# Modulation tiles issued from ScalarE's queue one turn ahead, with the offset row earlier and smaller recurrence masks

## The chip, the cores and the metric

The program runs on one core of one Trainium2 chip. Its engines are TensorE (PE; PEld is its weight load), VectorE (DVE), ScalarE (ACT), GpSimd (POOL) and SyncE (SP), which here only issues transfers. Each engine works through its own instructions in the order in which they stand, and waits at an instruction until what it needs is there. The metric is the device time of one execution in microseconds (us), the median of several runs.

## The reference

One layer of a transformer-like trunk, for a sequence of 2048 tokens of width 1024, in float32. A conditioning vector c gives six modulation vectors; the change touches how four of them are computed.

```python
mod = silu(c) @ ada_w + ada_b            # 1024 -> 6 x 1024
sh1, sc1, g1, sh2, sc2, g2 = split(mod, 6)
h = rmsnorm(x, norm_mix_w) * (1 + sc1) + sh1
proj = h @ w_in                          # 1024 -> 3624
o_a = hgrn2_mixer(...)                   # 4 heads, gated linear recurrence
o_b = dsa_mixer(...)                     # index scores, top 256 keys, softmax
o_c = conv_module(...)                   # 31 taps, depthwise
x = x + g1 * (concat([o_a, o_b, o_c]) @ w_out)
h = rmsnorm(x, norm_mlp_w) * (1 + sc2) + sh2
x = x + g2 * (square(relu(h @ w1)) @ w2)
out = rmsnorm(x, final_norm_w)
```

The recurrence `S_t = diag(f_t) S_(t-1) + (1 - f_t) outer i_t` is computed in pieces of 128 tokens; inside a piece the causal weights are built up over levels of halves (1, 2, 4, ... 64 tokens), and a mask says which entries each level writes.

## The kernel before

The sequence is cut into 4 blocks of 512 tokens. A matmul in float32 is made of three in a rounded format: high parts by high parts, and two cross terms (`mm_T`, L418 to L429). Weights come from HBM as `wraw`, are split into `whi` and `wlo`, and are kept in HBM (`wk_d`) for the blocks that follow, which load them as `wk`.

The program is written as a main stream of matmuls (`in_block`, `out_block`, `mlp_block`) with background work in generators: `queues` holds the recurrence ("fast"), the modulation ("ada"), the convolution ("conv"), the index scores, the top-k search and the attention. After each unit of the main stream `step` gives every queue a credit (`rates`, 800 for "ada"), and `pump` runs its generator until the credit is used up. The framework's scheduler then puts all instructions in an order of its own for each engine by a model of their durations, within what the tiles' buffers and dependences allow, and adds the waits. So an edit in one place can move instructions of every engine.

`ada_gen` (L770 to L785) computes g1, sc2, sh2 and g2 in 16 parts of 256 columns. A part has 8 turns (`ada_part`, L192 to L200). Each turn issues a transfer of a tile of 128 rows by 256 columns of `ada_w` from SyncE's queue (L195), and VectorE multiplies it by a column of silu(c) and adds it to the sum `acc` (L197 for the first, L199 after). The tiles have tag `adw` with AB = 2 buffers. For g1 and g2 a matmul with ones (L777) sums over the partitions; then the row of the offset is loaded, into the tag `adw` too (L779), added by VectorE (L780), which also frees the PSUM bank, and stored (L781). For sc2 and sh2 `ada_col` (L202 to L208) does it by columns. The queue is filled in block 1 and emptied at "prep" in block 3; the scheduler takes its first tiles earlier.

`ada_half` (L216 to L248) does the same for sc1 and sh1 at the very start, with tiles of 512 columns on SyncE's queue, since the first matmul needs them (a1 and sh1, used in `to_act_steps`, L286 to L291).

`late_consts` makes `lmask`, 5 levels by 256 entries of one byte: four equal copies of 64 entries, one for each piece of 128 tokens (L511 to L520). `hgrn_gen` reads it in `copy_predicated` at L690 and L711.

Of the kernel before, what the change touches and what calls it, by code (L numbers as in the profile page):

```python
# [8 lines left out]
F32 = mybir.dt.float32  # L9
# [3 lines left out]
U8 = mybir.dt.uint8  # L13
# [65 lines left out]
def trunk(ctx, tc, x, c, ada_w, ada_b, norm_mix_w, norm_mlp_w, w_in, hg_lb_logits,  # L79
# [22 lines left out]
    def nm(s):  # L102
        uid[0] += 1
        return f"{s}_{uid[0]}"
# [86 lines left out]

    def ada_part(pool, wtag, wbufs, acc, sec, c0, w):  # L192
        for k in range(NK):
            t = pool.tile([P, w], F32, tag=wtag, bufs=wbufs, name=nm("adw"))
            (nc.gpsimd if AQ else nc.sync).dma_start(t, ada2[k * P:(k + 1) * P, sec * D + c0:sec * D + c0 + w])  # L195
            if k == 0:
                V.tensor_scalar(acc, t, cact[:, 0:1], None, op0=OP.mult)  # L197
            else:
                V.scalar_tensor_tensor(acc, t, cact[:, k:k + 1], acc, op0=OP.mult, op1=OP.add)  # L199
            yield 1.2 * w  # L200

# [259 lines left out]
    lbt = cst.tile([P, 4], F32, name="lbt")  # L461
    lmask = cst.tile([P, 5, 256], U8, name="lmask")

# [31 lines left out]
    def late_consts():  # L495
# [16 lines left out]
        for l in range(5):  # L512
            h = 1 << l
            ng = 128 // (2 * h)
            V.memset(mwork, 1.0)
            G.affine_select(mwork, mwork, pattern=[[0, 4], [-2 * h, ng], [0, h]],
                            compare_op=OP.is_ge, fill=0.0, base=0, channel_multiplier=1)
            G.affine_select(mwork, mwork, pattern=[[0, 4], [2 * h, ng], [0, h]],
                            compare_op=OP.is_gt, fill=0.0, base=h, channel_multiplier=-1)
            V.tensor_copy(lmask[:, l, :], mwork)  # L520

# [155 lines left out]
    def hgrn_gen(b, h, q, k, f, v, gate):  # L677
# [8 lines left out]
        for i in range(2):  # L686
            pv = pd[i][:, :384].rearrange("p (c n) -> p c n", c=2)
            V.tensor_tensor(at.rearrange("p (c n) -> p c n", c=4)[:, 2 * i:2 * i + 2], pv[:, :, :P],
                            ident[:, None, :].to_broadcast([P, 2, P]), OP.mult)
            V.copy_predicated(at.rearrange("p (c g two) -> p c g two", c=4, two=2)[:, 2 * i:2 * i + 2, :, 1],  # L690
                              lmask[:, 0, :128].rearrange("p (c g) -> p c g", c=2), pv[:, :, P:])
        V.tensor_tensor(qn, qn, f.rearrange("p (c n) -> p c n", c=4), OP.mult)
# [4 lines left out]
        for l in range(7):  # L697
# [9 lines left out]
            if 0 < l < 5:  # L707
                for cc in range(4):
                    T.matmul(ps[:, cc * 64:(cc + 1) * 64], k[:, cc * P:(cc + 1) * P],
                             qv[:, cc, :, 1, :], start=True, stop=True)  # L710
                V.copy_predicated(av[:, :, :, 1, :],  # L711
                                  lmask[:, l, :].rearrange("p (c g e) -> p c g e", c=4, e=hs), psv)
            elif l:
# [56 lines left out]
    def ada_gen():  # L770
        for sec, dst in ((2, None), (4, a2), (3, sh2), (5, None)):
            for c0 in range(0, D, AW):
                acc = hp.tile([P, AW], F32, tag="ada", bufs=1, name=nm("adacc"))
                yield from ada_part(hp, "adw", AB, acc, sec, c0, AW)
                if dst is None:
                    pt = ps_xp(13)
                    T.matmul(pt[:1, :AW], ones, acc, start=True, stop=True)  # L777
                    row = hp.tile([1, AW], F32, tag="adw", bufs=AB, name=nm("adrow"))
                    dma(row, ada_b[0:1, sec * D + c0:sec * D + c0 + AW])  # L779
                    V.tensor_tensor(row, pt[0:1, :AW], row, OP.add)  # L780
                    dma(g_d[sec][:, c0:c0 + AW], row)  # L781
                else:
                    ada_col(acc, sec, c0, AW, dst)
            if sec == 4:
                ada_scale(a2, "nmlp")  # L785


# [892 lines left out]
```

## Time and profile before

| | before |
|---|---|
| median of 3 runs, us | 2964.3 (2963.78 to 2969.74) |
| the profiled execution, us | 2959.47 |
| its span, us | 2957.7 |
| mean granted TensorE clock | 0.981 |
| bytes moved | 688.62 MB, mean 233 GB/s |

The page gives busy time by engine, 40 slices of the span, the chain of work that ended last and the costliest groups. Other views of the same execution list groups of instructions with what ended the idle time before them, who waited for whom ("A <- B: us in total, times, longest us"), one tile's instructions with who waits for them, stretches with busy time of each engine, and instructions in order of time. SPq is SyncE's queue. An instruction is named by engine, line and tile (written <- read).

### The profile page before, as it was taken

To read this page: it belongs to the slowest core of one execution; us is meant where nothing else is said; L and a number is where in the kernel's file an instruction comes from. 1 tells how busy PE (TensorE), PEld (TensorE's weight loads), DVE (VectorE), ACT (ScalarE), POOL (GpSimd) and SP (SyncE) were. 2 spreads that over 40 slices of the span, in tenths; PEclk is the share of its full clock that TensorE was granted. 3 is DMA by queue.
4 is the path that set the end of the run, shared out by engine and by line. 5 is a ranking of instruction groups with operands and counts; after the bars stand their busy time and mean duration, and the time that the engine had idled before them with its cause. 6 is when DMAs were issued, how large, how long until landed. Compare 5 with 4: busy or idle time off the path is not lost.

```text
span 2957.7 us, 42853 instructions
## 1 busy us (share of the span) xinstructions
PE 2796.6 (95%) x14116; PEld 2310.3 (78%) x14116; DVE 1680.2 (57%) x3450; ACT 1297.0 (44%) x2704; POOL 1241.9 (42%) x1163
## 2 busy tenths in 40 slices
PE   6998988998899989999998999999999999999998
PEld 4877877787788877788776888877788888778777
DVE  7684486967526354756849637385944221244555
ACT  4545354545314235556545544444553333233333
POOL 7574152225205155566646322224432223335454
PEclk9999999899999999999998999999999999999999
DMA  8976666575655577899978967767786667676676
GB/s 283 289 232 220 214 218 214 175 226 180 213 183 179 177 239 249 266 281 307 300 233 263 299 193 221 225 217 237 246 286 210 224 207 229 214 272 229 224 228 214
DMA packets 428075, 688.62 MB, mean 233 GB/s; under 512 B 43383, under 2 KB 171452, under 8 KB 427836
## 3 DMA queue, kind: packets, MB, share of 16 engines
q1 hardware_dynamic: 427680, 685.67, 72.0%
q8 instruction: 113, 1.85, 0.3%
q14 instruction: 126, 1.03, 0.1%
q10 hardware_dynamic: 156, 0.07, 0.0%
HBM read 532.74 MB, written 152.84 MB: 232 GB/s over the span
## 4 chain that ended last, share of the span: by engine, by line
PE 38%; DMA 5%; DVE 4%; POOL 2%; issue 1%; ACT 1%; SPq 0%; POOLq 0%; DVEq 0%; ACTq 0%
PE mm L1317 10%; PE mm L427 8%; PE ax L427 6%; PE ax L1317 5%; PE mm L1477 4%; PE po L1013 1%; PE at L979 1%; PE at L1001 1%; DMA wk<-wk_d 1%; PE at L1317 1%; PE ix L822 1%; DMA tr<-in_mlp_w_dram 1%; DMA xo<-x_d 1%; DMA wraw<-in_mlp_w_dram 1%; DMA out_dram<-xo 1%
## 5 line engine op out<-in xcount | busy, mean ns | idle before, releaser
L427 PE MATMUL mm<-ah,wk 128*128 128x512 f32 x1920 | 517.3, 401 | 15.1 <-ACT k L647 5.9
L427 PEld LDWEIGHTS mm<-ah,wk 128*128 128x128 f32 x1920 | 358.3, 191 | 90.0 <-ACT k L647 6.9
L321 POOL TENSOR_TENSOR wlo<-wraw,whi 128x512 fp32r<-128x512 f32 x210 | 287.3, 1388 | 215.0 <-ACT whi L320 87.9
L1011 POOL TENSOR_TENSOR pT<-L,pT 128x512 fp32r<-128x512 f32 (+3 forms) x160 | 194.7, 1219 | 297.3 <-ACT pT L1010 183.1
L829 DVE SCALAR_TENSOR_TENSOR s<-r,iw_s,s 128x512 f32<-128x512 f32 (+3 forms) x266 | 239.2, 899 | 117.1 <-ACT r L824 108.8
L427 PE MATMUL mm<-al,wk 128*128 128x512 f32 x960 | 262.1, 395 | 0.0
L981 DVE CUSTOM_DVE_ANT_0 L<-at,bias 128x512 f32<-128x512 f32 (+3 forms) x152 | 93.4, 618 | 210.8 <-PE at L979 173.6
L427 PEld LDWEIGHTS mm<-al,wk 128*128 128x128 f32 x960 | 178.9, 190 | 36.0
L824 ACT ACTIVATE r<-ix 128x512 f32<-128x512 f32 (+3 forms) x256 | 133.4, 554 | 162.1 <-PE ix L822 117.1
L273 POOL TENSOR_TENSOR hl<-hr,hh 128x512 fp32r<-128x512 f32 x96 | 128.4, 1338 | 175.1 <-ACT hh L265 174.5
L1317 PE MATMUL mm<-wk,hh 128*128 128x512 f32 x640 | 198.1, 399 | 0.9 <-DVE ah L290 0.4
L598 POOL TENSOR_TENSOR cside<-cside,ctap 128x512 f32<-128x512 f32 x112 | 150.3, 1342 | 100.5 <-ACT ctap L597 88.3
L427 PE MATMUL ax<-ah,wk 128*128 128x512 f32 x720 | 187.0, 393 | 1.5 <-ACT hc L1451 1.5
L320 ACT CAST whi<-wraw 128x512 fp32r<-128x512 f32 x210 | 121.3, 620 | 146.7 <-DMA wraw<-in_mlp_w_dram 55.0
L931 DVE TENSOR_SCALAR_CACHE_REDUCE cum<-s,ssm 128x384 bf16<-128x384 f32 (+13 forms) x112 | 165.4, 1476 | 7.8 <-POOL s L833 5.7
L427 PEld LDWEIGHTS ax<-ah,wk 128*128 128x128 f32 x720 | 134.0, 188 | 31.2 <-ACT hc L1451 1.9
L1477 PE MATMUL mm<-wk,hc 128*128 128x512 f32 x588 | 148.3, 397 | 2.9 <-DVE acc L1485 2.8
L995 ACT ACTIVATE L<-L,nmx 128x512 f32<-128x512 f32 (+3 forms) x160 | 103.8, 650 | 105.8 <-DVE nmx L990 105.5
L1009 ACT COPY L<-at 128x512 f32<-128x512 f32 (+3 forms) x160 | 82.9, 522 | 152.0 <-PE at L1001 150.5
L1317 PEld LDWEIGHTS mm<-wk,hh 128*128 128x128 f32 x640 | 117.9, 188 | 27.1 <-DMA wk<-wk_d 0.9
L1477 PEld LDWEIGHTS mm<-wk,hc 128*128 128x128 f32 x588 | 109.5, 188 | 33.2 <-DVE acc L1485 6.7
L1317 PE MATMUL ax<-wk,hh 128*128 128x512 f32 x384 | 123.4, 400 | 0.9 <-DMA wk<-wk_d 0.5
(367 smaller groups left out, 6338.0 us busy)
## 6 DMA issues: line engine op xcount, KB each, us to landing
wk<-wk_d SPq DMA_DIRECT2D x776, 256.0 KB, 4.5
wk<-wk_d SPq DMA_DIRECT2D x196, 512.0 KB, 5.2
wk_d<-whi SPq DMA_DIRECT2D x210, 256.0 KB, 4.1
wk_d<-wlo SPq DMA_DIRECT2D x210, 256.0 KB, 5.7
wraw<-in_mlp_w_dram SPq DMA_DIRECT2D x68, 512.0 KB, 5.6
kc<-sk_d SPq DMA_DIRECT2D x112, 256.0 KB, 3.0
vc<-v_d SPq DMA_DIRECT2D x112, 256.0 KB, 4.9
adw<-in_ada_w_dram SPq DMA_DIRECT2D x128, 128.0 KB, 2.9
```

The costliest lines, as they stand in the source:

```text
L273: e.tensor_tensor(lo[:, i:j], src[:, i:j], hi[:, i:j].bitcast(F32), OP.subtract)
L320: A.copy(hi, src)
L321: G.tensor_tensor(lo, src, hi.bitcast(F32), OP.subtract)
L427: T.matmul(ps, ww[k], aa[k], start=(n == 0 and k0 == 0), stop=(n == len(order) - 1 and k1 == NK))
L598: G.tensor_tensor(side, side, tap, OP.add)
L824: A.activation(r[:, :w], ps[:, :w], AF.Relu, scale=32.0 ** -0.5)
L829: V.scalar_tensor_tensor(s[:, c0:c0 + w], r[:, :w], iw, s[:, c0:c0 + w], op0=OP.mult, op1=OP.add)
L931: V.tensor_scalar(dump, s, t, -AIM - i * STEP, op0=OP.is_ge, op1=OP.add, accum_out=d)
L995: A.activation(lt[:, :w], lt[:, :w], AF.Exp, bias=nmx, accum_out=sm[:, cb:cb + 1])
L1011: G.tensor_tensor(pT[:, :nt, 1], lv, pT[:, :nt, 0].bitcast(F32), OP.subtract)
L1317: T.matmul(ps, aa[f][:, tok * P:(tok + 1) * P], ww[i], start=(first and n == 0), stop=(last and n == 5))
L1477: T.matmul(bank[t], aa[:, k, t * P:(t + 1) * P], ww[k], start=(i in (0, 2, 4) and n == 0), stop=(n == 5), skip_group_check=True)
```

## The change

Three edits. The tiles of `ada_gen` are issued from ScalarE's queue (`nc.scalar.dma_start`), and the tile of the next turn is fetched before VectorE's operation of this one; the tag keeps its two buffers. The row of the offset gets a tag of its own (`adr`, one buffer), is issued from ScalarE's queue as well, and at the start of a part and not at its end. `lmask` holds 5 x 64 entries, which L690 and L711 read through a repeated index.

```diff
--- before.py
+++ after.py
@@ -189,15 +189,10 @@
     def col(key, i=0, n=1):
         return cols[:, offs[key] + i:offs[key] + i + n]
 
-    def ada_part(pool, wtag, wbufs, acc, sec, c0, w):
-        for k in range(NK):
-            t = pool.tile([P, w], F32, tag=wtag, bufs=wbufs, name=nm("adw"))
-            (nc.gpsimd if AQ else nc.sync).dma_start(t, ada2[k * P:(k + 1) * P, sec * D + c0:sec * D + c0 + w])
-            if k == 0:
-                V.tensor_scalar(acc, t, cact[:, 0:1], None, op0=OP.mult)
-            else:
-                V.scalar_tensor_tensor(acc, t, cact[:, k:k + 1], acc, op0=OP.mult, op1=OP.add)
-            yield 1.2 * w
+    def ada_fetch(sec, c0, k):
+        t = hp.tile([P, AW], F32, tag="adw", bufs=AB, name=nm("adw"))
+        nc.scalar.dma_start(t, ada2[k * P:(k + 1) * P, sec * D + c0:sec * D + c0 + AW])
+        return t
 
     def ada_col(acc, sec, c0, w, dst):
         n = w // P
@@ -459,7 +454,7 @@
     lbc = cst.tile([P, 4], F32, name="lbc")
     oml = cst.tile([P, 4], F32, name="oml")
     lbt = cst.tile([P, 4], F32, name="lbt")
-    lmask = cst.tile([P, 5, 256], U8, name="lmask")
+    lmask = cst.tile([P, 5, 64], U8, name="lmask")
 
     zq = cst.tile([P, 14], F32, name="zq")
     gq_ = cst.tile([P, 14], F32, name="gq_")
@@ -517,7 +512,7 @@
                             compare_op=OP.is_ge, fill=0.0, base=0, channel_multiplier=1)
             G.affine_select(mwork, mwork, pattern=[[0, 4], [2 * h, ng], [0, h]],
                             compare_op=OP.is_gt, fill=0.0, base=h, channel_multiplier=-1)
-            V.tensor_copy(lmask[:, l, :], mwork)
+            V.tensor_copy(lmask[:, l, :], mwork[:, :64])
 
     def ev_index_k(b, ps):
         full = st("stg", STG)
@@ -688,7 +683,7 @@
             V.tensor_tensor(at.rearrange("p (c n) -> p c n", c=4)[:, 2 * i:2 * i + 2], pv[:, :, :P],
                             ident[:, None, :].to_broadcast([P, 2, P]), OP.mult)
             V.copy_predicated(at.rearrange("p (c g two) -> p c g two", c=4, two=2)[:, 2 * i:2 * i + 2, :, 1],
-                              lmask[:, 0, :128].rearrange("p (c g) -> p c g", c=2), pv[:, :, P:])
+                              lmask[:, 0, None, :].to_broadcast([P, 2, 64]), pv[:, :, P:])
         V.tensor_tensor(qn, qn, f.rearrange("p (c n) -> p c n", c=4), OP.mult)
         yield 1500
         fl = f
@@ -709,7 +704,7 @@
                     T.matmul(ps[:, cc * 64:(cc + 1) * 64], k[:, cc * P:(cc + 1) * P],
                              qv[:, cc, :, 1, :], start=True, stop=True)
                 V.copy_predicated(av[:, :, :, 1, :],
-                                  lmask[:, l, :].rearrange("p (c g e) -> p c g e", c=4, e=hs), psv)
+                                  lmask[:, l, :].rearrange("p (g e) -> p g e", e=hs)[:, None].to_broadcast([P, 4, gc, hs]), psv)
             elif l:
                 for i in range(gc):
                     r0 = 2 * hs * i
@@ -768,22 +763,38 @@
     AW = 256
 
     def ada_gen():
-        for sec, dst in ((2, None), (4, a2), (3, sh2), (5, None)):
-            for c0 in range(0, D, AW):
-                acc = hp.tile([P, AW], F32, tag="ada", bufs=1, name=nm("adacc"))
-                yield from ada_part(hp, "adw", AB, acc, sec, c0, AW)
-                if dst is None:
-                    pt = ps_xp(13)
-                    T.matmul(pt[:1, :AW], ones, acc, start=True, stop=True)
-                    row = hp.tile([1, AW], F32, tag="adw", bufs=AB, name=nm("adrow"))
-                    dma(row, ada_b[0:1, sec * D + c0:sec * D + c0 + AW])
-                    V.tensor_tensor(row, pt[0:1, :AW], row, OP.add)
-                    dma(g_d[sec][:, c0:c0 + AW], row)
+        parts = [(sec, dst, c0) for sec, dst in ((2, None), (4, a2), (3, sh2), (5, None)) for c0 in range(0, D, AW)]
+        tiles = [(sec, c0, k) for sec, _, c0 in parts for k in range(NK)]
+        ahead = []
+
+        def fetch():
+            if tiles:
+                ahead.append(ada_fetch(*tiles.pop(0)))
+
+        fetch()
+        yield 1.2 * AW
+        for sec, dst, c0 in parts:
+            acc = hp.tile([P, AW], F32, tag="ada", bufs=1, name=nm("adacc"))
+            if dst is None:
+                row = hp.tile([1, AW], F32, tag="adr", bufs=1, name=nm("adrow"))
+                nc.scalar.dma_start(row, ada_b[0:1, sec * D + c0:sec * D + c0 + AW])
+            for k in range(NK):
+                t = ahead.pop(0)
+                fetch()
+                if k == 0:
+                    V.tensor_scalar(acc, t, cact[:, 0:1], None, op0=OP.mult)
                 else:
-                    ada_col(acc, sec, c0, AW, dst)
-            if sec == 4:
+                    V.scalar_tensor_tensor(acc, t, cact[:, k:k + 1], acc, op0=OP.mult, op1=OP.add)
+                yield 1.2 * AW
+            if dst is None:
+                pt = ps_xp(13)
+                T.matmul(pt[:1, :AW], ones, acc, start=True, stop=True)
+                V.tensor_tensor(row, pt[0:1, :AW], row, OP.add)
+                dma(g_d[sec][:, c0:c0 + AW], row)
+            else:
+                ada_col(acc, sec, c0, AW, dst)
+            if sec == 4 and c0 + AW == D:
                 ada_scale(a2, "nmlp")
-
 
     class TK:
         def __init__(self, pool, nmax, sbufs):
```

The numbers of VectorE's, GpSimd's and TensorE's instructions stay as they were; 136 transfers go from SyncE's to ScalarE's queue. The order of the rest is nearly the same, with exchanges of neighbours on all engines up to the middle of the program. Below are three places; a row has line, operation, written <- read and the size, with the line numbers of either kernel.

First place: VectorE near the start, where the sums for a1 and sh1 are made (L240 before, L235 after, 128x512; `adacc_248` and `adacc_285`). Before:

```order
L240 SCALAR_TENSOR_TENSOR adacc_248<-adw_263,cact,adacc_248 128x512
L504 TENSOR_TENSOR lbt<-cols 128x4
L520 CAST lmask<-mwork 128x256
L240 SCALAR_TENSOR_TENSOR adacc_248<-adw_266,cact,adacc_248 128x512
L438 TENSOR_SCALAR xt_212<-xt_212,rs_217 128x1024
L515 MEMSET mwork 128x256
L240 SCALAR_TENSOR_TENSOR adacc_248<-adw_269,cact,adacc_248 128x512
L506 RECIPROCAL lbc<-lbt 128x4
L438 TENSOR_SCALAR xt_221<-xt_221,rs_226 128x1024
L238 TENSOR_SCALAR adacc_285<-adw_287,cact 128x512
L240 SCALAR_TENSOR_TENSOR adacc_248<-adw_272,cact,adacc_248 128x512
```

After:

```order
L235 SCALAR_TENSOR_TENSOR adacc_248<-adw_263,cact,adacc_248 128x512
L499 TENSOR_TENSOR lbt<-cols 128x4
L785 TENSOR_SCALAR adacc_3821<-adw_3819,cact 128x256
L515 CAST lmask<-mwork 128x64
L433 TENSOR_SCALAR xt_212<-xt_212,rs_217 128x1024
L235 SCALAR_TENSOR_TENSOR adacc_248<-adw_266,cact,adacc_248 128x512
L510 MEMSET mwork 128x256
L787 SCALAR_TENSOR_TENSOR adacc_3821<-adw_3824,cact,adacc_3821 128x256
L235 SCALAR_TENSOR_TENSOR adacc_248<-adw_269,cact,adacc_248 128x512
L433 TENSOR_SCALAR xt_221<-xt_221,rs_226 128x1024
L501 RECIPROCAL lbc<-lbt 128x4
L233 TENSOR_SCALAR adacc_285<-adw_287,cact 128x512
```

The operations on the tiles of `ada_gen` (L785, L787) now stand between these sums; before, the first of them, L197, came after the last sum. The casts of `lmask` write 64 entries.

Second place: ScalarE in block 1, at the third group of columns of g1. `L` and `pT` belong to the attention, `csg`, `cside` and `ctap` to the convolution, `at_3048` to the recurrence. Before:

```order
L573 ACT_TABLE_LOAD
L573 ACTIVATE csg_4530<-mm_4496 128x512
L1009 COPY L_3635<-at_3644 128x256
L1010 CAST pT_3647<-L_3635 128x2x128
L721 COPY at_3048<-ax_3417 64x4x64
L995 ACT_TABLE_LOAD
L995 ACTIVATE L_3659,den_3744<-L_3659,nmx_3741 128x256
L733 COPY kt_3449<-ax_3444 128x512
L1022 COPY ot_3734<-po_3639 128x256
```

After:

```order
L568 ACTIVATE csg_4531<-mm_4497 128x512
L1006 ACT_TABLE_LOAD
L1006 ACTIVATE L_3635,den_3640<-L_3635,nmx_3637 128x256
L716 COPY at_3048<-ax_3417 64x4x64
L194 DMA adw_4555<-in_ada_w_dram 128x256
L194 DMA adw_4628<-in_ada_w_dram 128x256
L780 DMA adrow_4550<-in_ada_b_dram 1x256
L194 DMA adw_4631<-in_ada_w_dram 128x256
L194 DMA adw_4717<-in_ada_w_dram 128x256
L1020 COPY L_3635<-at_3644 128x256
L1021 CAST pT_3647<-L_3635 128x2x128
L728 COPY kt_3449<-ax_3444 128x512
```

Before, the copy of `L_3635` (L1009) and its cast came just ahead of that of `at_3048` (L721). After, `at_3048` (L716) comes first, then five transfers, then `L_3635` (L1020): two tiles, a row, two tiles. The last two tiles use the buffers of the first two, which VectorE's operations free.

Third place: SyncE around the same work, before. `wk` are weights, `kc` and `vc` keys and values of the attention.

```order
L195 DMA adw_4548<-in_ada_w_dram 128x256
L107 DMA wk_4567<-wk_d_1421 128x512
L107 DMA kc_3758<-sk_d_83 128x256
L107 DMA wk_4568<-wk_d_1421 128x512
L107 DMA mx_d_4_99<-ot_3619 128x128
L107 DMA mx_d_5_100<-ot_3619 128x128
L107 DMA wk_4569<-wk_d_1421 128x512
L107 DMA wk_4570<-wk_d_1421 128x512
L107 DMA kc_3864<-sk_d_83 128x256
L195 DMA adw_4551<-in_ada_w_dram 128x256
L107 DMA g_d<-adrow_4543 1x256
L195 DMA adw_4554<-in_ada_w_dram 128x256
```

The rows of L195 among the weight loads are gone after the change; the weight loads follow each other.

## The prediction

> **What bounds the kernel now.** I read the page first, for busy time by engine; then stretches of the span; then who waited for whom.
>
> ```profile
> span 2957.7 us, 42853 instructions
> PE 2796.6 (95%) x14116; PEld 2310.3 (78%) x14116; DVE 1680.2 (57%) x3450; ACT 1297.0 (44%) x2704; POOL 1241.9 (42%) x1163
> ```
>
> TensorE is busy for 95% of the span. 161.1 us are idle, and only these can shrink, since the change takes no matmul out. The tiles that it touches are issued by L195 from 38.1 to 745.2 us (row below), so I cut the span around that.
>
> ```profile
> 0.00:60.00 60.00, 32.43 (x144) 27.00 (x145) 44.74 (x87) 23.12 (x37) 45.08 (x46) 0.94 0.88 284
> 60.00:335.00 275.00, 252.57 (x1454) 217.08 (x1452) 177.45 (x428) 140.19 (x291) 144.41 (x140) 0.96 0.77 242
> 335.00:760.00 425.00, 388.33 (x2257) 327.75 (x2256) 311.57 (x764) 206.99 (x446) 142.71 (x158) 0.96 0.66 207
> ```
>
> The columns are the stretch, its length, busy time of PE, PEld, DVE, ACT and POOL, granted clock, DMA share and GB/s. In 335 to 760 us, where most tiles are loaded, TensorE idles 36.7 us. VectorE is busy 311.6 of 425 us, ScalarE 207.0, which leaves ScalarE 218 us. Some rows of what TensorE waited for there:
>
> ```profile
> PE mm L427 <- ACT k L647: 5.9, 2, 4.9
> PE mm L427 <- DVE adrow L780: 5.6, 3, 3.0
> PE ax L709 <- DVE k L675: 5.4, 6, 2.2
> PE at L822 <- DMA ki<-ki_d: 3.0, 2, 2.4
> PE mm L281 <- DVE gate L670: 0.2, 1, 0.2
> ```
>
> VectorE's late work leads, ScalarE's evictions stand beside it, and weights (wk) are in no row of that list. So a lighter weight queue is worth next to nothing, a VectorE that is less late something, and a later ScalarE costs.
>
> **VectorE's waits for the tiles.** Here lies what the change could win.
>
> ```profile
> L195 SPq DMA_DIRECT2D adw<-in_ada_w_dram x128: 327/333/1134, 38.1 to 745.2; - x128
> L199 DVE SCALAR_TENSOR_TENSOR adacc<-adw,cact,adacc x112: 400/484/1594, 54.0 to 750.3; 128x256 f32<-128x256 f32 x112
> L197 DVE TENSOR_SCALAR adacc<-adw,cact x16: 331/343/1170, 49.8 to 733.5; 128x256 f32<-128x256 f32 x16
>   DVE adacc L199: 70.3, 49
>   DVE adacc L197: 3.4, 2
> DMA to landing us min/median/max: 2.1/3.1/6.6
> ```
>
> VectorE waits 73.7 us for tiles in 51 places, 1.4 us each. A fetch one turn ahead seems to end that. But AB stays 2: a tile can be issued only when the operation on the tile two before it has freed the buffer, and from there an issue (0.33), a landing (3.1) and an operation (0.48) pass, some 3.9 us, before that buffer is free again. The old queue often stood at that limit:
>
> ```profile
> SPq L195 <- DMA adw<-in_ada_w_dram: 39.5, 33, 4.5
> SPq L195 <- DVE adacc L199: 38.7, 48, 2.3
> SPq L195 <- DVE nmx L990: 5.7, 4, 2.2
> SPq L195 <- DMA g_d<-adrow: 5.3, 6, 1.7
> SPq L195 <- DVE adacc L197: 4.7, 2, 4.2
> SPq L195 <- DMA wk<-wk_d: 4.6, 7, 1.5
> ```
>
> SyncE stood before L195 for 98.5 us in these rows, in 50 places because VectorE had not freed a buffer: those loads left as early as they could. So VectorE's waits stay nearly what they were. Their price: TensorE's waits of that stretch that VectorE released, adrow aside, are nine rows from 5.4 down to 0.2 us (first and last above), 17.3 us together. VectorE's own 311.6 us of work queue there too, so I charge half, 8.7 us, to the 73.7: 0.12 us of TensorE for a us of such short waits. Bounds are -8.7 us, if all go, and +5, if ScalarE issues late and they grow by 40 us. Taken: **-2 us**.
>
> **The row of the offset** comes eight turns earlier. Was it late?
>
> ```profile
> 373.12 0.25 SPq L107 DMA_DIRECT2D adrow<-in_ada_b_dram  x1
> 384.35 0.76 DVE L600 SCALAR_TENSOR_TENSOR cx<-hc,cvc,cx 128x512 f32<-128x512 f32 x1
> 385.02 0.41 DVE L780 TENSOR_TENSOR adrow<-mm,adrow 1x256 f32<-1x256 f32 x1
>   PE mm L777: 0.7, 1
> ```
>
> The row was issued 12 us before its use, VectorE came to it straight from L600, and the last line is all that VectorE ever idled before L780, once, for TensorE. TensorE's 5.6 us go back to VectorE's queue. **0 us**; bound -5.6.
>
> **ScalarE's new work decides.** 128 tile loads and 8 row loads leave SyncE's queue for ScalarE's. Issuing takes 128 x 0.333 + 8 x 0.25 = 44.6 us. The 98.5 us of waits, on a queue that had only transfers behind it, now stand before evictions, exponentials and casts, in order. Around 358 us (second place in the order above) five loads stand in a row between the copies L721 and L1009 (numbers of before). The fourth and fifth reuse the buffers of the first and second, so ScalarE must sit out a round trip of some 3.9 us, with L1009, the cast L1010 and, for TensorE, the bank that L1009 empties behind it. This trace has such stalls:
>
> ```profile
> 507.25 0.27 ACT L565 CAST v<-mm 128x128 fp32r<-128x128 f32 x1 [5.41 <-DVE ssm L940]
> 509.32 0.59 ACT L647 ACTIVATE k<-mm 128x512 f32<-128x512 f32 x1
> PE mm L427 <- ACT k L647: 11.5, 3, 5.6
> ACT v L565 <- DMA v_d<-v: 17.0, 5, 4.9
> ```
>
> ScalarE stood 5.41 us, the eviction L647 came after, and TensorE waited. Between 60 and 760 us such waits are 11.5 us, against stalls before L565 of 22.4 us (17.0 and 5.41): 0.51 us for a us, where stalls near 5 us hit an eviction. Most of the new ones are short, 98.5 us over 128 loads or 0.8 us, so VectorE's price of 0.12 is the nearer row: (44.6 + 98.5) x 0.12 = 17 us. Bounds are 0, if ScalarE's idle half absorbs all of it, and 98.5 x 0.51 + 44.6 x 0.12 = 56 us. Taken: **+17 us**.
>
> SyncE sheds the same 143 us. Only ki (3.0 us) was waited for: **-2 us**, bounds -3 and 0. If ScalarE stalls long enough for weights to be late behind its loads, that cover is gone.
>
> The Trainium skill, "DMA: Bandwidth & Descriptors", section "Issuing engines are not separate DMA queues", says that DMAs of all issuing engines share the same 16 DMA engines, so that spreading them saves the sequencer's time alone. By that rule the sum would be the ki row, -2 us; the trace agrees that SyncE's time is not what TensorE waits for, but the rule leaves out what the new issuer loses.
>
> **The start** has VectorE and the DMA engines nearly full:
>
> ```profile
> 13.00:49.00 36.00, 22.77 (x105) 18.88 (x106) 33.43 (x50) 13.08 (x21) 26.16 (x23) 1.00 1.02 317
> L520 DVE CAST lmask<-mwork x5: 279/294/1351, 6.5 to 31.1; 128x256 uint8<-128x256 f32 x5
> 66.76 1.91 DVE L199 SCALAR_TENSOR_TENSOR adacc<-adw,cact,adacc 128x256 f32<-128x256 f32 x2
> 68.70 0.68 DVE L527 TENSOR_TENSOR kst<-stg,kst 32x512 fp32r<-32x512 f32 x1
> 75.49 0.73 PE L427 MATMUL mm<-ah,whi 128*128 128x512 f32 x2 [2.95 <-DVE slo L540]
> ```
>
> In the new order (first place above) six operations on modulation tiles come before the last partial sums of a1 and sh1: 0.343 + 5 x 0.484 = 2.8 us, where VectorE idled 2.6 of 36 us. Four smaller lmask casts return at most 4 x 0.294 = 1.2 us. So the matmuls after sh1 come some 2 us later. Against that, kst no longer stands behind 1.91 us of these operations, and on its store hangs the buffer behind the wait of 2.95 us at 75.49. Taken: **0 us**, bounds -2 and +4.
>
> **The masks** keep their values.
>
> ```profile
> L711 DVE COPY_PREDICATED at<-lmask,ax x64: 406/437/742, 109.8 to 1111.4; 128x256 f32<-128x256 uint8 x64
> L690 DVE COPY_PREDICATED at<-lmask,ax x32: 420/438/451, 101.8 to 1090.5; 128x128 f32<-128x128 uint8 x32
> ```
>
> Element counts stay; only the mask is read repeatedly. Were that as slow per element as L690 (3.4 ns against 1.7), 64 copies would take 28 us more of VectorE, 3.4 us at 0.12. Nothing here shows such a slowing: **0 us**, bounds 0 and 3.4.
>
> **Sum:** -2 + 0 + 17 - 2 + 0 + 0 = +13 us. The profiled execution took 2959.47 us (its span and 1.77 us around it), so 2972.5 us; the median of the runs shown is 2964.3, 4.8 us above it, and on that footing the forecast is **2977 us**. The reordering of all engines up to some 1100 us can move single waits either way; 6 us, about the longest in the lists, covers it.
>
> **Rivals.** (1) *Faster: the tiles land sooner on a queue of their own.* Now they sit among weights on one queue. If all landed in 2.1 us, the minimum, 51 waits would shrink by 1.0 us each, VectorE by 51 us and TensorE by 6; with ScalarE's stalls hidden in its 218 idle us and ki, that is -8, or 2956 us. For it: half of ScalarE is idle, and landing varies from 2.1 to 6.6. Against it: DMA share is 0.66 there, transfers still meet, and the round trip over two buffers stays. It decides from where ScalarE's price falls under 0.05. Chance 0.28. The Trainium skill, "DMA: Bandwidth & Descriptors", section "Queues, rings and completion order", has each DMA engine go round robin between queues, packet by packet, which is this rival's cause; that no run here yet shows. (2) *No change: ScalarE absorbs it*, VectorE's waits stay, the sum is about -4 to +5: 2964 us, chance 0.20. (3) *Much slower: long stalls before evictions*, as at 358 us, at the price of 0.51 for half of the 98.5 us: 0.51 x 49 + 0.12 x 94 = 36 us, so 3000 us, chance 0.12. The forecast, +6 to +25 us, keeps 0.40.
>
> **How the numbers follow.** A measurement of this kernel can tell some 0.2% (6 us) from no change. Faster is rival 1 (0.28), same is rival 2 (0.20), slower is the forecast and rival 3 (0.52). The range runs from 2952, where VectorE's -8.7 and ki's -3 meet a free ScalarE, to 3000, rival 3; the rest of rival 3 and a gain on the row besides are left out.
>
> **What would show it.** ScalarE's waits before adw loads near 100 us; VectorE's waits for adw still above 50 us; TensorE's waits for ScalarE in 335 to 760 us up by 10 us or more; adrow rows unchanged; the wait at 75.49 shorter. The forecast is wrong if VectorE's waits for adw fall below 25 us while TensorE's for ScalarE stay under 15.

## The result, and the profile after

The changed kernel takes 2993.0 us (median of 4 runs, 2986.94 to 3001.3) where the kernel before takes 2967.0 beside it: ratio 1.0089, 95% interval 1.0068 to 1.011. It is slower by 26 us; the forecast was 13. Its profiled execution took 2986.94 us with this head (page of the changed kernel: span, then busy time, share and instructions of each engine):

```profile
span 2984.9 us, 42882 instructions
PE 2804.7 (94%) x14116; PEld 2319.0 (78%) x14116; DVE 1684.5 (56%) x3450; ACT 1293.2 (43%) x2704; POOL 1242.1 (42%) x1163
```

The span grew by 27.2 us. TensorE's busy time grew by 8.1 with the same 14116 matmuls, and its idle time from 161.1 to 180.2 us. Busy time follows the granted clock (0.981 on average in the profiled execution of before, 0.976 here), and that varies from run to run as well (last section). So below I compare idle time, from one trace for each kernel. The same stretches as before, in the changed kernel:

```profile
0.00:60.00 60.00, 29.56 (x129) 24.56 (x130) 44.41 (x88) 21.32 (x34) 42.27 (x44) 0.92 0.85 282
60.00:335.00 275.00, 256.18 (x1492) 220.14 (x1491) 179.48 (x437) 141.60 (x296) 149.35 (x144) 0.98 0.79 248
335.00:760.00 425.00, 377.02 (x2158) 316.68 (x2157) 300.98 (x735) 203.78 (x441) 140.37 (x156) 0.94 0.64 198
```

Idle time of TensorE is the length less the first busy time. It is 30.4 us in the first stretch (27.6 before), 18.8 in the second (22.4) and **48.0 us in 335 to 760 us, where it was 36.7**. This stretch holds most of the loss; the rest, 8.5 us, lies scattered behind 760 us, where idle time differs as much between kernels that take the same time (table behind run 12). What TensorE waited for there (line, releaser, us in total, times, longest):

```profile
PE at L1036 <- POOL ot L1034: 10.8, 7, 4.3
PE po L1024 <- POOL pT L1022: 5.2, 3, 3.2
...
PE ax L704 <- DVE k L670: 3.4, 3, 1.6
PE at L833 <- DMA ki<-ki_d: 3.1, 1, 3.1
...
PE mm L422 <- DVE adrow L792: 1.8, 2, 1.3
...
PE mm L422 <- ACT k L642: 0.5, 1, 0.5
```

The evictions of the linear layers (5.9 us before) are no longer in front; in their place stand GpSimd's parts of the attention output, 16.0 us in two rows, of which before had 0.9. The longest of these waits, 4.3 us, has ScalarE's loads behind it. Rows of four engines in order of time (start, us, engine, operation, idle time before it and releaser):

```profile
506.36 0.48 DVE L787 SCALAR_TENSOR_TENSOR adacc<-adw,cact,adacc 128x256 f32<-128x256 f32 x1 [2.16 <-DMA adw<-in_ada_w_dram]
506.88 0.34 ACTq L194 DMA_DIRECT2D adw<-in_ada_w_dram  x1
507.26 1.08 ACT L835 ACTIVATE r<-at 128x512 f32<-128x512 f32 x2 [3.44 <-DVE ssm L951]
508.23 0.38 ACT L1033 COPY ot<-po 128x256 f32<-128x256 f32 x1
508.69 0.51 POOL L1034 TENSOR_TENSOR ot<-ot 128x128 f32<-128x128 f32 x1 [7.39 <-ACT ot L1033]
509.25 0.48 PE L1036 MATMUL at<-ident,ot 128*128 128x128 f32 x1 [4.26 <-POOL ot L1034]
```

VectorE waits for a tile; its operation frees a buffer at 506.84; the next load, which stood for that buffer, leaves at 506.88; then come ScalarE's operations, GpSimd's and TensorE's. ScalarE's idle 3.44 us end with the load, though the row names another operation of VectorE. By the same views loads for which ScalarE stood come shortly before some 7 of the 16.0 us; before other long waits in these two rows (3.18 us at 688.47, 1.81 at 713.99, 1.56 at 378.92) it stood at none. Nor does a long stall have to cost much, as a second place shows:

```profile
640.90 5.36 ACTq L194 DMA_DIRECT2D adw<-in_ada_w_dram  x4
646.30 0.37 ACT L1033 COPY ot<-po 128x256 f32<-128x256 f32 x1 [10.14 <-PE mm L422]
646.57 0.60 ACT L568 ACTIVATE csg<-mm 128x512 f32<-128x512 f32 x1
650.21 1.32 ACTq L194 DMA_DIRECT2D adw<-in_ada_w_dram  x2
651.57 0.37 ACT L1037 ACTIVATE ot<-at,rd 128x128 f32<-128x128 f32 x1 [4.40 <-DVE adacc L787]
```

```profile
646.75 0.46 POOL L1034 TENSOR_TENSOR ot<-ot 128x128 f32<-128x128 f32 x1 [10.05 <-ACT ot L1033]
647.26 0.33 PE L1036 MATMUL at<-ident,ot 128*128 128x128 f32 x1 [0.29 <-POOL ot L1034]
```

Four loads stand in a row in ScalarE's order from 640.90 on, behind a fifth that left at 635.96; each of the four leaves when VectorE has freed its buffer. The copy `ot` stands behind them, GpSimd behind the copy. ScalarE is idle for 10.14 us, the longest of its stalls at loads, and TensorE, which had other matmuls, for 0.29. Such stalls are what I had forecast. Whether they are the cause is another matter, and the experiments say that they alone are not.

VectorE's side (groups on the tiles, and its waits for their loads):

```profile
L194 ACTq DMA_DIRECT2D adw<-in_ada_w_dram x128: 334/335/389, 9.8 to 755.3; - x128
L787 DVE SCALAR_TENSOR_TENSOR adacc<-adw,cact,adacc x112: 356/484/1536, 18.1 to 761.0; 128x256 f32<-128x256 f32 x112
  DVE adacc L787: 83.3, 46
```

Its waits grew from 73.7 to 83.3 us in 46 places, instead of going away. The masks cost what they did (437 and 438 ns before):

```profile
L706 DVE COPY_PREDICATED at<-lmask,ax x64: 416/438/752, 109.5 to 1132.2; 128x256 f32<-128x256 uint8 x64
L685 DVE COPY_PREDICATED at<-lmask,ax x32: 426/436/449, 100.6 to 1108.4; 128x128 f32<-128x128 uint8 x32
```

### The profile page after: what moved, and what is told of

It is laid out like the page before. It is cut to its first block, busy times and chain, and to the rows that moved or that the text cites. A ratio compares the mean times of both kernels' runs of the same rounds, so it can differ in the third digit from the quotient of the medians.

```text
span 2984.9 us, 42882 instructions
## 1 busy us (share of the span) xinstructions
PE 2804.7 (94%) x14116; PEld 2319.0 (78%) x14116; DVE 1684.5 (56%) x3450; ACT 1293.2 (43%) x2704; POOL 1242.1 (42%) x1163
## 4 chain that ended last, share of the span: by engine, by line
PE 41%; DMA 4%; DVE 2%; POOL 2%; issue 1%; ACT 1%; SPq 0%; POOLq 0%; DVEq 0%; ACTq 0%
PE mm L1328 10%; PE mm L422 9%; PE ax L422 7%; PE ax L1328 5%; PE mm L1488 4%; PE po L1024 1%; PE at L990 1%; PE at L1012 1%; PE ix L833 1%; DMA wk<-wk_d 1%; PE at L1328 1%; DMA wraw<-in_mlp_w_dram 1%; DMA ki<-ki_d 1%; DMA tr<-in_mlp_w_dram 1%; POOL wk L374 1%
## 5 line engine op out<-in xcount | busy, mean ns | idle before, releaser
L1020 ACT COPY L<-at 128x512 f32<-128x512 f32 (+3 forms) x160 | 82.9, 522 | 175.6 <-PE at L1012 157.0
```

## The experiments

Each kernel ran against the kernel before on the same chip. Beside the ratio I give TensorE's idle time in 335 to 760 us (36.7 before, 48.0 in the changed kernel) from the row of that stretch; the table behind run 12 sets it beside the rest of the span.

**1. The loads back on SyncE.** Edit to the changed kernel:

```diff
-        nc.scalar.dma_start(t, ada2[k * P:(k + 1) * P, sec * D + c0:sec * D + c0 + AW])
+        nc.sync.dma_start(t, ada2[k * P:(k + 1) * P, sec * D + c0:sec * D + c0 + AW])
-                nc.scalar.dma_start(row, ada_b[0:1, sec * D + c0:sec * D + c0 + AW])
+                nc.sync.dma_start(row, ada_b[0:1, sec * D + c0:sec * D + c0 + AW])
```

> The changed kernel with its tile loads and row loads issued by SyncE again; the fetch one turn ahead, the row's own tile and the small masks stay. Theory A (ScalarE's queue: 44.6 us of issues and some 100 us of waits stand before evictions, casts and exponentials): the loss goes, 2960 to 2972 us, and VectorE's waits for the tiles stay above 50 us, since two buffers remain. Rival B (the look-ahead moves operations on tiles into the start and reorders VectorE's queue): the loss stays, 2985 to 3000 us. Rival C (the masks, read four times, or the row): the loss stays too, as in B.

Measured: 2974.0 us, ratio 1.0017 (1.0002 to 1.0033), 2 us above theory A's range and far below that of the others. Its row of the stretch, and VectorE's waits:

```profile
335.00:760.00 425.00, 393.32 (x2240) 333.32 (x2240) 313.52 (x765) 205.73 (x446) 144.61 (x159) 0.94 0.66 206
```

```profile
  DVE adacc L787: 67.6, 53
```

31.7 us of idle time in the stretch (this trace is the slowest of the kernel's 12 runs, and has 15 us more than before's behind 760 us). By the medians the queue alone makes 0.72% of the 0.89%, some 21 us. With two buffers the look-ahead leaves VectorE's waits at 67.6 us (73.7 before), as the prediction had argued.

**2. The queue alone.** Edit to the kernel before:

```diff
-            (nc.gpsimd if AQ else nc.sync).dma_start(t, ada2[k * P:(k + 1) * P, sec * D + c0:sec * D + c0 + w])
+            (nc.gpsimd if AQ else nc.scalar).dma_start(t, ada2[k * P:(k + 1) * P, sec * D + c0:sec * D + c0 + w])
```

> The kernel before with one word changed: the modulation tiles are issued by ScalarE; no look-ahead, the row from SyncE as before, masks as before. Theory A (ScalarE's queue): nearly the whole loss appears, 2985 to 3000 us. Rival B (look-ahead and reordering): 2960 to 2972 us. Rival D (queue and look-ahead each cost nothing, only together, because runs of several loads stand in a row in ScalarE's order): 2960 to 2975 us here and in the run with the loads on SyncE.

Measured: 2992.1 us, 1.0090 (1.0063 to 1.0117). One word brings the whole loss, with no look-ahead, row or mask. The stretch:

```profile
335.00:760.00 425.00, 380.57 (x2187) 319.36 (x2186) 307.49 (x751) 200.06 (x440) 141.41 (x157) 0.96 0.65 200
```

44.4 us of idle time. The six runs had a mean clock of 0.9735, the 29 of before beside them 0.9765; a straight line through those 29 gives 1.6 us for 0.001, so by this estimate some 5 us of the difference go with the clock, by chance or not. Theory A holds so far, B and D fall.

**3. The masks alone**, in the kernel before.

```diff
-    lmask = cst.tile([P, 5, 256], U8, name="lmask")
+    lmask = cst.tile([P, 5, 64], U8, name="lmask")
-                              lmask[:, 0, :128].rearrange("p (c g) -> p c g", c=2), pv[:, :, P:])
+                              lmask[:, 0, None, :].to_broadcast([P, 2, 64]), pv[:, :, P:])
```

> The kernel before with the small masks alone, each read four (or two) times. Theories A and B: no change, 2960 to 2972 us, the masked copies at 437 and 438 ns as before. Rival C: up to 28 us of VectorE and some +3 us for TensorE or more. It is also a measure of what a change with no weight of its own does through the scheduler's reordering: theory A expects less than 6 us of that.

Measured: 2967.3 us, 0.9995 (0.9981 to 1.0009). Nothing, as forecast; rival C falls as to the masks (the row is run 11).

**4. Three buffers on ScalarE's queue.** Edit to the changed kernel (the row pays for the space):

```diff
-WQ, AQ, AB = 0, 0, 2
+WQ, AQ, AB = 0, 0, 3
-                row = hp.tile([1, AW], F32, tag="adr", bufs=1, name=nm("adrow"))
...
+                row = hp.tile([1, AW], F32, tag="adw", bufs=AB, name=nm("adrow"))
```

> The changed kernel with three tile buffers where it has two; the row goes back to its late place in the tiles' buffers, which pays for the third. Queue still ScalarE's, fetch still one turn ahead. Theory A with the buffer round trip as the cause of ScalarE's waits: ScalarE's waits before the tile loads that VectorE releases shrink to less than half, VectorE's waits for tiles (83 us) fall below 50 us, and some 10 to 20 of the 26 us come back: 2970 to 2985 us. If ScalarE's waits come from landings instead (the semaphores shared with other transfers) or from issuing alone, they stay and the time stays at 2985 to 3000 us.

Measured: 2968.9 us, 1.0007 (0.9987 to 1.0027): the loss is gone, more than I expected. VectorE's waits:

```profile
  DVE adacc L784: 49.0, 39
```

So 128 issues on ScalarE, some 45 us, don't make the loss. Nor do its stalls by themselves: they did not shrink to less than half, as I had expected, but only to two thirds (67.0 us by the count in run 10, 100.9 in the changed kernel). The row went back to its late place here too, so the third buffer alone is run 5 against run 2.

**5. The same without look-ahead:** the kernel before with the small masks of run 3, the word of run 2 and `AB = 3`.

> The kernel before with its tile loads on ScalarE's queue and three tile buffers, paid for by the small masks; no look-ahead, the row late and on SyncE as before. Theory A1 (on ScalarE's queue the loss is the waits that two buffers cause, since a load stands until VectorE has freed a buffer): 2965 to 2976 us, like the changed kernel with three buffers. Theory A2 (the loss is the issuing and whatever else ScalarE's queue does, and three buffers only helped together with the look-ahead): 2985 to 3000 us, like the queue alone.

Measured: 2967.3 us, 1.0005 (0.9992 to 1.0018). The third buffer cures the queue with the look-ahead and without; A1 holds, A2 falls.

**6. Every other tile on ScalarE**, two buffers (the row on SyncE):

```diff
-        nc.scalar.dma_start(t, ada2[k * P:(k + 1) * P, sec * D + c0:sec * D + c0 + AW])
+        (nc.scalar if k % 2 else nc.sync).dma_start(t, ada2[k * P:(k + 1) * P, sec * D + c0:sec * D + c0 + AW])
```

> The changed kernel with the odd tiles issued by ScalarE and the even ones, and the row, by SyncE: 64 loads on ScalarE where it has 128, two buffers. If the loss is proportional to the loads on ScalarE: half of it, about 13 us over the loads on SyncE, 2980 to 2988 us. If it comes from loads that stand in a row in ScalarE's order (the third waits for the round trip of the first): almost gone, 2970 to 2978 us.

Measured: 2979.5 us, 1.0046 (1.0033 to 1.0059). That is 0.29% over run 1, where the changed kernel is 0.72% over it: some 40% of the loss for half the loads, between my two ranges, so it decides neither. Idle time in the stretch is 37.5 us, against 31.7 in run 1:

```profile
335.00:760.00 425.00, 387.48 (x2215) 325.67 (x2214) 303.95 (x761) 199.17 (x442) 142.47 (x157) 0.94 0.65 203
```

This kernel also shows the same transfer from two queues (issues, KB each, median us to landing):

```profile
adw<-in_ada_w_dram SPq DMA_DIRECT2D x64, 128.0 KB, 3.0
adw<-in_ada_w_dram ACTq DMA_DIRECT2D x64, 128.0 KB, 3.5
```

The trace has the landing of only 8 and 9 of the 64 loads each, so these medians are weak. Matching loads and operations says the same with more cases: where VectorE waits for a tile, its operation starts 3.1 us (median of 28) after the issue from SyncE and 4.2 us (of 21) after that from ScalarE. From ScalarE's queue a tile comes about 1 us later there.

**7. GpSimd's queue:** both loads of run 1 from `nc.gpsimd` instead.

> The changed kernel with tiles and rows issued by GpSimd, two buffers, fetch one turn ahead. If the loss belongs to any engine that works in order and has a chain to TensorE (GpSimd makes wlo, cside, ot and x): 2980 to 3005 us. If it belongs to ScalarE alone, because it empties TensorE's banks: 2965 to 2978 us, as with the loads on SyncE.

Measured: 2971.5 us, 1.0022 (1.0011 to 1.0033), as on SyncE. Yet GpSimd stood long before these loads (its issues, and its waits before them):

```profile
L194 POOL DMA_DIRECT2D adw<-in_ada_w_dram x128: 538/556/767, 1.6 to 744.5; - x128
  POOL adw L194: 115.9, 67
```

128 x 0.556 = 71 us of issuing and 115.9 us of waiting, more than ScalarE's, cost nothing to be seen. Of the three queues tried only ScalarE's makes the loss.

**8. Three buffers on SyncE:** run 4 with the loads of run 1.

> The changed kernel with three tile buffers (the row back at its late place to pay for the third), tiles and row on SyncE. Against the changed kernel with three buffers on ScalarE this leaves only the queue apart. By my price of 0.12 us of TensorE for a us of VectorE's short waits: VectorE's waits for tiles fall from 68 to below 45 us, worth some 3 us, and ScalarE's issues, 45 us, some 5 us more: 2958 to 2968 us. If three buffers make the queue free altogether: 2964 to 2974 us, as on ScalarE.

Measured: **2956.2 us, 0.9968 (0.9958 to 0.9979)**, the only kernel of the study faster than before, by some 10 us, and below both of my ranges. VectorE's waits and the stretch, with 27.9 us of idle time:

```profile
  DVE adacc L784: 40.6, 29
```

```profile
335.00:760.00 425.00, 397.06 (x2337) 336.46 (x2336) 318.01 (x772) 209.79 (x455) 151.62 (x163) 0.96 0.68 213
```

Against run 4 the queue alone is worth 0.39%, 12 us, still. Against run 1 two things differ, the third buffer and the late row.

**9. Three buffers on SyncE without look-ahead:** the kernel before with the small masks and `AB = 3`.

> The kernel before with three tile buffers (paid for by the small masks) and nothing else: tiles and row from SyncE, no look-ahead. If the third buffer alone makes the gain of the run with three buffers on SyncE: 2952 to 2962 us, VectorE's waits for tiles near 41 us. If the look-ahead is needed for it: 2962 to 2970 us. Against the run with three buffers on ScalarE and no look-ahead (+0.05%) it gives the price of ScalarE's queue with three buffers: 8 to 13 us by the pair with look-ahead.

Measured: 2966.7 us, 1.0008 (0.9991 to 1.0025). VectorE's waits are as short as in run 8:

```profile
  DVE adacc L199: 41.9, 29
```

In time nothing is gained, and the price of run 5 to this one is none. That doesn't make the 32 us of shorter waits worthless. Up to 760 us TensorE idles 76.9 us here and 75.2 in run 8, against 86.7 before, and behind 760 us, where no tile is loaded, this kernel gives back 11.4 of them and run 8 5.3 (table behind run 12). Whether run 8's gain needs the look-ahead is therefore not shown; the look-ahead with two buffers and a late row wasn't run.

**10. Small loads on ScalarE instead of the tiles.** Tiles and rows as in run 1; each turn takes its column of the activation from a copy in memory:

```diff
+        cact_d = dram([P, 8], F32, "cact_d")
+        dma(cact_d, cact)
...
+                c1 = hp.tile([P, 1], F32, tag="cc", bufs=3, name=nm("cc"))
+                nc.scalar.dma_start(c1, cact_d[:, k:k + 1])
-                    V.scalar_tensor_tensor(acc, t, cact[:, k:k + 1], acc, op0=OP.mult, op1=OP.add)
+                    V.scalar_tensor_tensor(acc, t, c1, acc, op0=OP.mult, op1=OP.add)
```

> The changed kernel with tiles and rows back on SyncE, and on ScalarE's queue 128 small loads in their place: each turn's column of the activation (128 x 1) is loaded from a copy in memory into one of three buffers, and VectorE's operation on the tile takes it from there. ScalarE issues as many loads as in the changed kernel and waits before them for VectorE's operations, while the tiles come as early as SyncE can. Against the run with tiles on SyncE (+0.17%, 2974 us): if the loss of the change is what ScalarE's own work loses by issues and waits, 10 to 20 us more, 2980 to 2992 us; if it is the tiles' landing later for VectorE, no more than 5 us, 2970 to 2979 us, with VectorE's waits for tiles and columns together near 70 us.

Measured: 2975.1 us, 1.0022 (1.0002 to 1.0042), as run 1. ScalarE issued as often and stood nearly as long. Some of its waits, those that the view puts down to VectorE's operations on tiles or to a load of a tile or column, from 60 to 765 us (16 rows of 68.4 us, first and last):

```profile
ACT ot L1037 <- DVE adacc L791: 11.6, 3, 8.7
...
ACT L639 <- DVE adacc L791: 0.7, 1, 0.7
```

In the changed kernel the like are 8 rows of 46.9 us:

```profile
ACT ctap L592 <- DVE adacc L787: 11.5, 4, 4.5
...
ACT ot L1033 <- DVE adacc L787: 2.0, 1, 2.0
```

These rows miss stalls that are put down to something else, as both places of the changed kernel above. So I took from the traces, for every group of loads in ScalarE's order, the time from the end of the operation before it to the end of its last issue (60 to 765 us). In the changed kernel this is 142.8 us, 100.9 of them waiting and the rest issuing; here 134.6 us, 91.0 of them waiting. A stall of 8.7 us stands before the same copy `ot`. Nine tenths of ScalarE's stalls, and no loss over run 1: they are by themselves not what costs. My first theory falls here.

**11. The row alone:** the kernel before with the small masks and the row in a tile of its own, issued eight turns ahead by SyncE.

> The kernel before with the row of the offset alone changed (its own tile, issued eight turns ahead, on SyncE; the small masks pay for the space): two buffers, no look-ahead. My prediction put 0 us on it, with a bound of -5.6: 2960 to 2970 us. If the row, out of the tiles' buffers, frees them for a tile: 2955 to 2962 us. If it is the early row that makes the run with tiles on SyncE 5 us slower: 2970 to 2976 us.

Measured: 2979.0 us, 1.0049 (1.0032 to 1.0067), above all three ranges. I had put nothing on it. Idle time in the stretch is 35.5 us, no more than before:

```profile
335.00:760.00 425.00, 389.49 (x2193) 329.79 (x2192) 310.01 (x746) 202.10 (x439) 145.38 (x158) 0.92 0.65 202
```

The loss isn't where the row is used. In the whole span idle time is 7 us above before's profiled execution (168.2 against 161.1): 4.4 less up to 760 us and 11.4 more behind, where neither tile nor row is loaded. The granted clock was 0.974 on average in its 7 runs (0.976 in the 22 of before beside it). Run 1, which has the early row too, lost only 0.17%, so the parts don't add up; what makes the time behind 760 us longer was not found.

**12. The small loads with two buffers:** run 10 with `bufs=2` for the columns.

> The run with the small loads on ScalarE, with two buffers for them where it had three; the tiles stay on SyncE. With three buffers the small loads cost no more than the loads on SyncE alone (+0.22% beside +0.17%), though ScalarE's stalls were there. New theory F: the loss is not what ScalarE's own work loses, but that VectorE waits for a load that stands behind ScalarE's work, and two buffers give no lead to cover it. Then two buffers make VectorE's waits over 2 us rise from 36 towards the changed kernel's 60 us, by the small loads, and the loss comes back: 2983 to 2995 us. Theory A (ScalarE's stalls themselves): they are the same with two buffers as with three, so 2970 to 2980 us as before.

Measured: 2969.5 us, 1.0005 (0.9992 to 1.0018): no loss, against my new theory. VectorE's waits, by what ended them:

```profile
  DMA adw<-in_ada_w_dram: 51.1, 22
  DMA cc<-cact_d: 26.6, 23
```

Together 77.7 us, as in run 2, but only 26.6 of them for loads that ScalarE issued. Theory F in its simple form, that VectorE's longer waits are the loss, falls. The run did not bring the dose for its other half: VectorE waiting 80 us for ScalarE's loads.

**Where TensorE's idle time lies.** All tile loads are issued by 760 us. Idle time (length less busy time of TensorE) up to there and behind, one trace for each kernel:

| kernel | loads on ScalarE, buffers | up to 760 us | behind 760 us | ratio |
|---|---|---|---|---|
| changed | tiles, 2 | 97.2 | 82.9 | 1.0089 |
| run 2 | tiles, 2 | 97.7 | 81.5 | 1.0090 |
| run 6 | half the tiles, 2 | 89.2 | 82.9 | 1.0046 |
| before | none, 2 | 86.7 | 74.5 | 1 |
| run 12 | small, 2 | 86.4 | 78.8 | 1.0005 |
| run 7 | none (GpSimd), 2 | 85.2 | 80.1 | 1.0022 |
| run 10 | small, 2 | 84.5 | 82.5 | 1.0022 |
| run 1 | none, 2 | 83.1 | 89.6 | 1.0017 |
| run 11 | none, 2 | 82.3 | 85.9 | 1.0049 |
| run 3 | none, 2 | 81.7 | 76.6 | 0.9995 |
| run 5 | tiles, 3 | 79.2 | 81.2 | 1.0005 |
| run 4 | tiles, 3 | 78.7 | 86.8 | 1.0007 |
| run 9 | none, 3 | 76.9 | 85.9 | 1.0008 |
| run 8 | none, 3 | 75.2 | 79.8 | 0.9968 |

(In the second column the number is that of buffers for the tiles, in run 12 also for the small loads; run 10 has three of those.) Up to 760 us the kernels stand nearly in the order of what was changed: ScalarE's queue with two buffers costs some 11 to 16 us; a third buffer saves 5 to 12 on SyncE's queue and 18 on ScalarE's; with three buffers ScalarE's queue costs 2 to 4. Behind 760 us the idle time lies between 74 and 90 us in no such order, and the kernel before has the least. None of the moved loads is there, so the reordering is the likeliest cause of this spread; that was not tested. The boundary is one of time, not of work, so these are rough sums.

## Why the prediction was right or wrong

**What was shown.** The loss is the tile loads on ScalarE's queue with two buffers: the queue alone makes all of it (run 2), half the loads make some 40% (run 6), a third buffer takes it away (run 5 against run 2, and run 4), to within 0.4% of the like kernel on SyncE; and neither the masks (run 3), nor another engine's queue that works in order (run 7), nor the same number of loads on ScalarE with nearly the same stalls (runs 10 and 12) make it. Every one of these edits also changes the scheduler's order, and run 11, with a row that VectorE had never waited for, is 12 us slower. The 25 us that come with one word and go with one buffer (and the small masks, worth nothing by run 3) are twice that; differences of some 10 us between single kernels, those of runs 6 and 8 among them, could be the order by the times alone.

**The step that fell short** is "ScalarE's new work decides", +17 us. By its size it is the right term: 21 us (changed kernel over run 1) to 27 us (run 2), inside its bounds of 0 to 56. It was made of 143 us of issues and waits at 0.12 us each. The 143 us were right (142.8 by the count in run 10, the waits 100.9 where I charged 98.5), but the price has no ground in the runs. As many issues with 91.0 us of waits cost 0.05% where the tiles came from SyncE (run 10 against run 1), and with 67.0 us left the loss was gone (run 4). So the product came near the truth by a wrong route, and that is luck. That TensorE's waits for ScalarE would rise by 10 us was wrong word for word: its rows of ScalarE in 335 to 760 us fell from 9.8 to 5.3 us (the eviction `k` from 5.9 to 0.5), and the rise stands in the rows of GpSimd, with ScalarE's loads behind some 7 of the 16.0 us.

**VectorE's waits,** -2 us: that two buffers keep them was right (run 1: 67.6 us). That they would grow was only in the bound of +5, for late issues. From the trace, with each load matched to its operation: in the changed kernel a load leaves 0.2 us on average after its buffer came free (0.6 in run 1), so ScalarE does not issue late. But where VectorE waits, the operation starts 4.2 us (median) after the end of the issue, against 2.9 in run 1 and in the kernel before, and 3.7 in run 2. The waits are fewer and longer: 21 over 2 us with 59.7 us in all, against 10 with 31.1 before and 9 with 29.5 in run 1. That alone is not the loss either: run 2 has 14 with 46.5 us and run 12, which lost nothing, 13 with 44.9; and by the same count GpSimd's loads take 4.1 us and those of runs 4 and 5 3.9 and 4.0 without a like loss.

**What stays open** is how the longer landing, the two buffers and ScalarE's order work together. One reading fits most of the runs, and the chain at 506 to 509 us above shows it once: VectorE waits for a load that stands in ScalarE's order, ScalarE's next load waits for VectorE, and the two engines hold each other up by turns. VectorE's waits for loads issued by ScalarE are 83 us in the changed kernel and 79 in run 2 (loss over the like kernel with its loads on SyncE or GpSimd: 0.72 and 0.90%), 49 and 46 in runs 4 and 5 (0.39 and none), 32 in run 6 (0.29), 27 and 4 in runs 12 and 10 (none). Runs 5 and 6 are out of order in this, and it is no proof: in each of the seven kernels the scheduler also wrote another order. What would settle it, the written order held fixed while the queue alone changes, wasn't tried.

**The row,** 0 us: in the changed kernel its own wait fell from 5.6 to 1.8 us, within the bound, but alone it cost 12 us (run 11), which no bound of mine held. **The reordering** was given 6 us for single waits; run 11 moved by 12 us with no other cause that the trace shows, so it may be worth about twice that, and the parts don't add. **SyncE's shedding,** -2 us: `ki` still costs 3.1 us; nothing came of it. **The start,** 0 us: TensorE idles 2.8 us more up to 60 us and 3.6 us less up to 335, which is inside -2 to +4. The wait at 75.49 us is gone, as I had said. **The masks,** 0: shown (run 3).

**The rivals.** (1) had the tiles land sooner on a queue of their own; they come later (4.2 against 3.1 us from issue to use in one kernel, run 6). The rule of the Trainium skill that I put beside it, in "DMA: Bandwidth & Descriptors", section "Queues, rings and completion order" (engines serve their queues in turn), does not tell which queue fares better; in run 6 tiles come sooner from the busier one. (2), ScalarE absorbs it, is about what happens with three buffers. (3), long stalls before evictions, gave 3000 us; the time came within 7 us of it, but run 10 has stalls of that length without the loss. The same page, section "Issuing engines are not separate DMA queues", would have given -2 us: that spreading the issues saves little agrees with run 7 (0.05% from run 1), and what it leaves out, 21 to 27 us on ScalarE, depends on the buffers.

## What to carry to other kernels

Before a load is moved to a compute engine's queue, count the buffers behind it: with a round trip of 4 to 5 us over two buffers the move to ScalarE lost 0.7 to 0.9%, with three 0.4% or nothing, and the move to GpSimd nothing to be seen. A look-ahead without a buffer for it does little: with two buffers VectorE's waits went from 73.7 to 67.6 us, with three to 41 us with or without it. Read a change first in the stage that it touches: the third buffer saved idle time up to 760 us in all four kernels that had it, and only one of them came out faster. And a stall that can be seen in the timeline is not yet a cost: put the same stall there by other means, and see whether the time follows.

## What the runs showed of the hardware

The granted clock varied between runs of one and the same kernel: over 29 runs of before on one chip it went from 0.970 to 0.979, and the times from 2958.3 to 2977.3 us. The slowest run had 0.970 and the fastest 0.978, but one at 0.978 took 2974.7 us, so the mean clock explains only a part. The profiled execution of before, with 0.981, was a lucky one: 2959.5 us, where 2967 is the median. A comparison of two single executions can be 10 us off by that alone. TensorE's idle time leaves the clock out, but it isn't shown to be steadier: there is one trace for each kernel, and that of run 1 idles 11.6 us more than before's where the medians differ by 5 us.
